# The second layer's experts with weights in 8 KB runs, gate and up on the two halves of the array, and the features stored in that order

## The chip, the cores and the metric

The kernel runs on one core of one Trainium2 chip. The metric is the device time of one launch in microseconds (us), as the median of the runs shown. All data is fp32 in DRAM; products run on TensorE (PE), elementwise work on VectorE (DVE), ScalarE (ACT) and GpSimd (POOL), and loads are issued from SyncE's queue (SP).

## What is computed

A backbone of two layers: each mixes tokens by four kinds of attention and then passes them through a hierarchical mixture of 16 gated experts, of which every token uses two. The second layer handles 256 latent tokens. What matters here is its mixture:

```python
eid = grp[:, None] * EXPERTS_PER_GROUP + top_i          # two experts of a token
gate = jnp.einsum('nke,nk->ne', one_hot(eid, N_EXPERTS), w_top)
y = jnp.zeros(hf.shape)                                 # hf: (256, 1024), normed, scaled and shifted
for e in range(N_EXPERTS):                              # 16
    a = silu(hf @ w_gate[e]) * (hf @ w_up[e])           # w_gate, w_up: (1024, 512)
    y = y + gate[:, e:e + 1] * (a @ w_down[e])          # w_down: (512, 1024)
```

The weights of one layer's experts are 16 x 3 x 2 MB, and each is read once.

## The kernel before, in words

`moe(l, ...)` holds the mixture of a layer; the second layer takes the path `half`. Its weights are read as 96 tiles of 1 MB into a ring of 15 places (`RING[1]`), in the order of the list `todo` (L1145 to L1149): gate in two tiles (the first and the second 512 of its 1024 rows), up in two, then down of the expert before in two. `load_expert` (L1120) issues each as one DMA on SP: row 128k + p of the tile goes to partition p as its k-th piece, so that a partition takes runs of 2 KB (a row of gate or up) or 4 KB (a row of down). A DMA is issued once its place in the ring is free.

The tokens, normed but not yet scaled and shifted, are kept as two float32r parts `xhat` (L1224 on ACT, L1225 and L1226 on POOL). `half_experts` (L1475) works on them. `tables` (L1491), for four experts at a time, gathers the tokens of each expert by products with one-hot rows (L1505), applies scale and shift feature by feature (`modulate`, L264 and L266, with `mod2`), and leaves `X`, feature-major, with room for 64 tokens an expert; L1511 makes the tokens' weights and L1519 the transposed one-hot rows.

`expert` (L1539) is a generator with these steps, all of PE's work in fp32:

- gate and up (L1547): per 128 features, X's 64 tokens are the stationary operand and weights the moving one; columns 0 to 255 go to the lower half of the array, columns 256 to 511 to the upper half, so that a product is 64 x 256, 32 of them an expert;
- SiLU on ACT (L1551) and the product with up on DVE (L1552), 128 x 256 each;
- two transposes of 128 x 128 (L1556) and a copy on ACT (L1558);
- down (L1564): 8 products of 64 x 512, again with halves of the columns on halves of the array; then weighting on DVE (L1567) and a split in two float32r parts (L1569 on ACT, L1570 on DVE);
- the combining products (L1576), 8 of 128 x 512, which add the expert's rows to the tokens' sums in PSUM.

The loop at L1592 interleaves experts: gate of e, combine of e-2, up of e, down of e-1, transposes of e. Then a scheduler with its own estimate of durations orders the instructions of each engine; the order on PE, fixed at build time, is thus neither the loop's nor the programmer's. After the last expert a norm follows and the output is stored (L1697 to L1711).

In the trace a fp32 product of PE is recorded as two MATMUL instructions, so that "x16" in a row of the trace is 8 products of the program.

## Time and profile before

| | us |
|---|---|
| runs shown | 1304.49, 1299.95, 1298.3 (median 1299.95) |
| profiled execution, span from first to last instruction | 1302.6 |
| second layer's experts, first table product to the last combining product | 1043.3 to 1289.8 |
| PE busy | 1146.7 (88%) |
| DVE busy | 793.7 (61%) |
| ACT busy | 559.1 (43%) |
| POOL busy | 254.3 (20%) |

The page gives the profiled execution's span and no separate device time for it; the span lies between the three runs, 2.65 us above their median. The profile is read here mostly by its timeline: start of a merged run of like instructions, its length, engine, line, operation, tiles, shape and count. A run's length contains the draining of its last product, so that the time a run takes up on PE is read from its start to the next run's start.

### The profile page before, as it was taken

What the parts mean: (1) busy time and instruction counts of PE and PEld (TensorE: products, weight loads), DVE (VectorE), ACT (ScalarE), POOL (GpSimd) and SP (SyncE); (2) the same over time, 40 slices, a digit from 0 to 9 for tenths busy, and PEclk for the clock granted to TensorE, in tenths of its full rate; (3) what the DMA queues carried; (4) which work ended last, traced back from release to release, by engine and by line L of the source; (5) the groups of instructions that cost most, each with busy time, mean ns of one, the idle gap of its engine ahead of it and who ended that gap; (6) DMA issues with size and microseconds to landing.
All of it is one profiled execution on the core that took longest, in us unless ns stands there. A gap on an engine that the chain in (4) does not pass through costs nothing. (4 is left out here: it accounts for less than half of the span.)

```text
span 1302.6 us, 16444 instructions
## 1 busy us (share of the span) xinstructions
PE 1146.7 (88%) x5920; PEld 770.1 (59%) x5920; DVE 793.7 (61%) x1676; ACT 559.1 (43%) x951; POOL 254.3 (20%) x235
## 2 busy tenths in 40 slices
PE   5999999899945999989999978998989589999995
PEld 2777644367833777767777647654457455455552
DVE  4377156674797899979888688735874711211113
ACT  2332155664325677767677444415553311111110
POOL 0022011222132344435352205120001200000000
PEclk9999969989967899999999979997979789999998
DMA  9933546701567899999998453542723979999993
GB/s 351 311 106 83 188 171 236 241 12 34 202 226 250 284 328 346 336 330 352 307 319 276 175 176 119 153 162 106 259 84 101 329 244 395 393 394 394 394 394 138
DMA packets 151770, 315.77 MB, mean 242 GB/s; under 512 B 21295, under 2 KB 36405, under 8 KB 146560
## 3 DMA queue, kind: packets, MB, share of 16 engines
q1 hardware_dynamic: 146868, 305.96, 66.9%
q0 software_dynamic: 4560, 8.57, 1.8%
q8 instruction: 49, 0.80, 0.3%
q14 instruction: 41, 0.34, 0.1%
q10 hardware_dynamic: 252, 0.09, 0.0%
HBM read 307.28 MB, written 15.27 MB: 248 GB/s over the span
## 5 line engine op out<-in xcount | busy, mean ns | idle before, releaser
L1360 DVE TENSOR_TENSOR hl<-rb,hl 128x1024 fp32r<-128x1024 f32 x127 | 189.7, 1520 | 30.6 <-ACT hl L1358 30.3
L1358 ACT ACTIVATE hl<-rb 128x1024 fp32r<-128x1024 f32 x152 | 158.0, 1058 | 69.8 <-PE mm L1370 63.3
L1370 PE MATMUL mm<-hl,t 128*128 128x512 f32 x256 | 106.0, 414 | 3.2 <-DVE hl L1360 3.2
L1371 PE MATMUL mm<-hl,t 128*128 128x512 f32 x256 | 102.9, 402 | 4.5 <-DVE t L1389 4.3
L1369 PE MATMUL mm<-hl,t 128*128 128x512 f32 x256 | 103.0, 407 | 1.1 <-ACT t L1388 1.1
L1547 PE MATMUL mm<-rb,xt 128*64 128x256 f32 x816 | 101.0, 383 | 0.0
L563 PE MATMUL mm<-s,hh 128*128 128x512 f32 x216 | 88.1, 412 | 0.0
L565 PE MATMUL mm<-s,hh 128*128 128x512 f32 x216 | 87.9, 410 | 0.0
L564 PE MATMUL mm<-s,hh 128*128 128x512 f32 x216 | 87.0, 403 | 0.0
L1547 PEld LDWEIGHTS mm<-rb,xt 128*64 128x64 f32 x816 | 58.1, 137 | 35.3 <-issue 8.8
L1360 POOL TENSOR_TENSOR hl<-rb,hl 128x1024 fp32r<-128x1024 f32 x25 | 70.1, 2815 | 24.2 <-ACT hl L1358 23.5
L824 ACT ACTIVATE e<-mm,nmx 128x512 f32<-128x512 f32 (+1 forms) x96 | 58.4, 616 | 29.3 <-DVE nmx L819 16.3
L819 DVE TENSOR_REDUCE nmx<-mm 128x1 f32<-128x512 f32 (+1 forms) x80 | 52.7, 684 | 11.1 <-PE mm L813 10.3
L1371 PEld LDWEIGHTS mm<-hl,t 128*128 128x128 f32 x256 | 49.7, 194 | 16.2 <-DVE t L1389 6.7
L1370 PEld LDWEIGHTS mm<-hl,t 128*128 128x128 f32 x256 | 49.7, 194 | 14.7 <-DVE hl L1360 5.2
L1552 DVE TENSOR_TENSOR ta<-ta,mm 128x256 f32<-128x256 f32 x16 | 6.7, 421 | 84.4 <-ACT ta L1551 84.4
L1369 PEld LDWEIGHTS mm<-hl,t 128*128 128x128 f32 x256 | 49.7, 194 | 12.1 <-ACT t L1388 2.0
L1369 PE MATMUL mm<-hl,at 128*128 128x512 f32 x128 | 53.0, 414 | 3.7 <-ACT at L1408 3.7
L1371 PE MATMUL mm<-hl,at 128*128 128x512 f32 x128 | 50.2, 411 | 6.0 <-DVE at L1409 5.7
L833 POOL TENSOR_SCALAR e<-e,rc 128x256 f32<-128x256 f32 x32 | 30.0, 950 | 128.7 <-DVE rc L831 98.5
L1370 PE MATMUL mm<-hl,at 128*128 128x512 f32 x128 | 52.9, 413 | 1.5 <-DVE hl L1360 1.2
L424 ACT ACTIVATE s<-ra 128x1024 fp32r<-128x1024 f32 x30 | 31.3, 1059 | 51.4 <-PE mm L565 25.5
(494 smaller groups left out, 2437.4 us busy)
## 6 DMA issues: line engine op xcount, KB each, us to landing
rb<-in_moe_w_up_dram SPq DMA_DIRECT2D x52, 1024.0 KB
rb<-in_moe_w_down_dram SPq DMA_DIRECT2D x50, 1024.0 KB
rb<-in_moe_w_gate_dram SPq DMA_DIRECT2D x49, 1024.0 KB
ra<-in_w_ada_dram SPq DMA_DIRECT2D x40, 1024.0 KB
ra<-in_moe_w_gate_dram SPq DMA_DIRECT2D x14, 1024.0 KB
ra<-in_w_in_dram SPq DMA_DIRECT2D x24, 512.0 KB
ra<-in_moe_w_down_dram SPq DMA_DIRECT2D x11, 1024.0 KB
ra<-in_moe_w_up_dram SPq DMA_DIRECT2D x9, 1024.0 KB
```

The costliest lines, as they stand in the source:

```text
L424: S.activation(hi, w, AF.Copy)
L563: T.matmul(ps, a, hi[:, k2], start=k == 0, stop=False)
L564: T.matmul(ps, a, lo[:, k2], start=False, stop=False)
L565: T.matmul(ps, b, hi[:, k2], start=False, stop=k == KD - 1)
L819: V.tensor_reduce(nmx[:, :nb], ps, axis=AX, op=ALU.max, negate=True)
L824: S.activation(e[:, b], ps[:, b], AF.Exp, bias=nmx[:, b:b + 1], accum_out=sm[:, b:b + 1])
L1358: S.activation(hi, w[k2], AF.Copy)
L1360: eng.tensor_tensor(lo, w[k2], hi.bitcast(F32), op=ALU.subtract)
L1369: T.matmul(ps[:C], ah, hs[:, k2], start=first and k2 == 0, stop=False)
L1370: T.matmul(ps[:C], ah, ls[:, k2], start=False, stop=False)
L1371: T.matmul(ps[:C], al, hs[:, k2], start=False, stop=last and k2 == 1)
L1547: T.matmul(ps[64 * t:64 * t + 64, j], X[:, k, gi], wt, start=k == 0, stop=k == KD - 1)
```

## The change

The tile of gate or up now puts rows 4p to 4p+3 of its 512 into partition p, one run of 8 KB; down puts rows 2p and 2p+1 of its 256 there, also 8 KB. The contraction index of a product is thereby another set of features, so the features of `xhat` are stored in that order (ACT and POOL write or read with a step of 128 elements), scale and shift get a third copy `mod2[:, 2]` in that order (a 4 x 512 load and four small transposes, once), and the activations' columns are taken with a step of 2 in the transposes. Gate now works on the lower half of the array and up on the upper half, both over all 512 columns: 16 products of 64 x 512 an expert instead of 32 of 64 x 256, and the load order is gate, up, gate, up. SiLU and the product with up are 64 x 512 instead of 128 x 256; four transposes of 64 x 128 take the place of two of 128 x 128. Cut to its core (comments and the path for overfull experts, which does not run, left out):

```diff
-        V.tensor_copy(mod2, ps[:, 0:32].rearrange("p (s r) -> p s r", s=2))
+        V.tensor_copy(mod2[:, 0:2], ps[:, 0:32].rearrange("p (s r) -> p s r", s=2))
         V.tensor_copy(lnb, ps[:, 32:40])
+        if not full:
+            r4 = P3("r4", [4, 512])
+            SY.dma_start(r4, modD[l][0:1, 1024:3072].rearrange("s (r p) -> (s r) p", p=512))
+            ps = tr([128, 4, 4])
+            for j in range(4):
+                T.transpose(ps[:, j], r4[:, j::4], ident[0:4, 0:4])
+            V.tensor_copy(mod2[:, 2].rearrange("p (r j) -> p j r", j=4), ps)
...
-            src = src.rearrange("(k p) n -> p k n", p=128)
+            src = src.rearrange("(p k) n -> p k n" if half else "(k p) n -> p k n", p=128)
...
-            for n, d in (("gate", 0), ("up", 0), ("down", 1)) if half else (("up", 1), ("gate", 0), ("down", 1)):
+            if half:
+                todo += [(e, f"moe_w_{n}", i) for i in range(2) for n in ("gate", "up") if e < E]
+                todo += [(e - 1, "moe_w_down", i) for i in range(2) if e > 0]
+                continue
+            for n, d in (("up", 1), ("gate", 0), ("down", 1)):
...
-                    S.activation(xhat[0][:, ch], x, AF.Identity, scale=rstd2[:, c:c + 1], bias=nb[:, c:c + 1])
+                    hi, lo = (t[:, ch].rearrange("p (h j q) -> p h q j", h=2, j=4) for t in xhat)
+                    xv, xhv = (t.rearrange("p (h q j) -> p h q j", h=2, j=4) for t in (x, xh))
+                    S.activation(hi, xv, AF.Identity, scale=rstd2[:, c:c + 1], bias=nb[:, c:c + 1])
                     G.tensor_scalar(xh, x, rstd2[:, c:c + 1], nb[:, c:c + 1], op0=ALU.mult, op1=ALU.add)
-                    G.tensor_tensor(xhat[1][:, ch], xh, xhat[0][:, ch].bitcast(F32), op=ALU.subtract)
+                    G.tensor_tensor(lo, xhv, hi.bitcast(F32), op=ALU.subtract)
...
-                ps = mm([128, 2, 256])
-                for j, n in enumerate(("moe_w_gate", "moe_w_up")):
-                    for kh in range(2):
-                        for kt, wt in enumerate(pieces(e, n, kh)):
-                            k, t = 4 * kh + kt // 2, kt % 2
-                            T.matmul(ps[64 * t:64 * t + 64, j], X[:, k, gi], wt, start=k == 0, stop=k == KD - 1)
-                    if j == 0:
+                ps = mm([128, 512])
+                for kh in range(2):
+                    both = [pieces(e, f"moe_w_{n}", kh) for n in ("gate", "up")]
+                    for k in range(4 * kh, 4 * kh + 4):
+                        for t in range(2):
+                            T.matmul(ps[64 * t:64 * t + 64], X[:, k, gi], next(both[t]),
+                                     start=k == 0, stop=k == KD - 1)
+                    if kh == 0:
                         yield
-                a = PX("ta", [128, 256], bufs=2)
-                S.activation(a, ps[:, 0], AF.Silu)
-                V.tensor_tensor(a, a, ps[:, 1], op=ALU.mult)
+                a = PX("ta", [64, 512], bufs=2)
+                S.activation(a, ps[0:64], AF.Silu)
+                V.tensor_tensor(a, a, ps[64:128], op=ALU.mult)
                 yield
-                pt = tr([128, 2, 128])
-                for k in range(2):
-                    T.transpose(pt[:, k], a[:, 128 * k:128 * k + 128], ident)
-                aT = PX("at", [128, 2, 128], bufs=2)
+                pt = tr([128, 4, 64])
+                for k in range(4):
+                    T.transpose(pt[:, k], a[:, 256 * (k // 2) + k % 2:256 * (k // 2) + 256:2], ident[0:64, 0:64])
+                aT = PX("at", [128, 4, 64], bufs=2)
```

The scheduler also orders PE's instructions anew. The first place is PE in the last four experts, where one expert follows another with nothing else between. In the rows `mm` is the sum of gate and up, `mx` that of down; `rb`, `ra` and `x` are weight tiles; `y` and `ohT` belong to the combining products and `tr<-cst,ta` are the transposes; "x8" is a count of products. Before, around the gate and up products of expert 13 (`mm_10826`), from the last combining product of expert 12 on:

```order
L1576 MATMUL mm_9255<-y_10818,ohT_10195 128x512
L1547 MATMUL mm_10826<-rb_2498_10651,xt_10525 64x256 x8
L1547 MATMUL mm_10826<-rb_2499_10657,xt_10525 64x256 x8
L1547 MATMUL mm_10826<-ra_10675,xt_10525 64x256 x8
L1564 MATMUL mx_10878<-ra_10685,at_10824 64x512 x4
L1556 MATMUL tr_10895<-cst,ta_10875 128x128 x2
L1564 MATMUL mx_10878<-rb_2508_10703,at_10824 64x512 x4
L1547 MATMUL mm_10900<-rb_2509_10713,xt_10525 64x256 x8
L1576 MATMUL mm_9252<-y_10891,ohT_10581 128x512
```

With the change, from the transposes of expert 12 into the products of expert 13 (`mm_10606`):

```order
L1572 MATMUL tr_10599<-cst,ta_10577 128x64 x4
L1580 MATMUL mx_10580<-x_2480_10441,at_10542 64x512 x4
L1562 MATMUL mm_10606<-rb_2481_10444,xt_10347 64x512
L1591 MATMUL mm_9260<-y_10595,ohT_10073 128x512
...
L1562 MATMUL mm_10606<-rb_2484_10457,xt_10347 64x512
L1562 MATMUL mm_10606<-rb_2481_10444,xt_10347 64x512
L1562 MATMUL mm_10606<-rb_2484_10457,xt_10347 64x512
```

Before, eight products of an expert (four on each half of the array) stand between the down products of the expert before it and that expert's eight combining products, and 24 stand behind these. Now one product (gate's first, on the lower half) stands ahead and 15 stand behind, which begin with one on the upper half (`rb_2481` holds gate, `rb_2484` up).

The second place is PE while the tables of the last four experts are made (`tr<-oh,xhat`). Before:

```order
L1505 MATMUL tr_10537<-oh_10516,xhat_7864 128x256
L1547 MATMUL mm_10598<-x_2444_10347,xt_10139 64x256 x8
L1547 MATMUL mm_10598<-rb_2451_10365,xt_10139 64x256 x7
L1505 MATMUL tr_10526<-oh_10516,xhat_7863 128x256
L1505 MATMUL tr_10526<-oh_10516,xhat_7864 128x256
```

With the change:

```order
L1519 MATMUL tr_10359<-oh_10338,xhat_7863 128x256
L1519 MATMUL tr_10359<-oh_10338,xhat_7864 128x256
L1562 MATMUL mm_10420<-x_2430_10195,xt_10017 64x512
L1519 MATMUL tr_10348<-oh_10338,xhat_7863 128x256
L1519 MATMUL tr_10348<-oh_10338,xhat_7864 128x256
```

A run of 15 products between table products has become a run of one. Over all 16 experts the runs of gate and up products, taken between products of other lines, number 50 with 512 products before, 16 of them of an odd count, and 46 with 256 products now, 32 of them of an odd count. Down has 24 runs before and 26 now, two of an odd count in each. Changes of kind on PE, with down and gate or up in a row counted as one kind, number 126 before and 119 now.

## Rows read from the trace of the kernel before

**Rows 1.** Page, part 1: busy time, share of the span and instructions of each engine.

```profile
PE 1146.7 (88%) x5920; PEld 770.1 (59%) x5920; DVE 793.7 (61%) x1676; ACT 559.1 (43%) x951; POOL 254.3 (20%) x235
```

**Rows 2.** Stretches: us; busy of PE, PEld, DVE, ACT, POOL; PE clock; DMA share; GB/s.

```profile
1010.00:1020.00 10.00, 5.74 (x28) 4.69 (x27) 7.98 (x20) 3.68 (x6) 0.00 (x0) 0.86 1.04 386
1090.00:1270.00 180.00, 177.03 (x1261) 97.06 (x1260) 32.59 (x68) 26.90 (x60) 0.00 (x0) 1.00 1.04 394
1270.00:1275.00 5.00, 4.88 (x42) 2.90 (x42) 0.69 (x1) 0.18 (x1) 0.00 (x0) 1.00 1.03 411
1275.00:1280.00 5.00, 5.00 (x36) 2.23 (x34) 0.42 (x1) 0.77 (x2) 0.00 (x0) 1.00 0.67 270
```

**Rows 3.** Who PE waited for, 1046 to 1290 us: us in total, times, longest.

```profile
PE tr L1556 <- DVE ta L1552: 4.0, 3, 1.9
PE mm L1576 <- ACT y L1569: 1.6, 1, 1.6
```

**Rows 4.** Timeline of PE in expert 12: start, us, line, tiles, shapes, count.

```profile
1231.25 1.90 PE L1547 MATMUL mm<-rb,xt 128*64 128x256 f32 x16
1233.08 1.38 PE L1576 MATMUL mm<-y,ohT 64*128 64x512 f32 x8
1234.39 5.40 PE L1547 MATMUL mm<-rb,xt 128*64 128x256 f32 x48
1239.62 1.89 PE L1564 MATMUL mx<-rb,at 128*64 128x512 f32 x8
1241.44 0.44 PE L1556 MATMUL tr<-cst,ta 128*128 128x128 f32 x2
1241.80 1.94 PE L1564 MATMUL mx<-x,at 128*64 128x512 f32 x8
1243.57 1.90 PE L1547 MATMUL mm<-rb,xt 128*64 128x256 f32 x16
```

**Rows 5.** Timeline of PE, one product alone between two runs of combining products.

```profile
1081.51 0.65 PE L1547 MATMUL mm<-rb,xt 128*64 128x256 f32 x2
1082.08 0.73 PE L1576 MATMUL mm<-y,ohT 64*128 64x512 f32 x4
```

**Rows 6.** Timeline of PE, products with one column and their 128-column loads.

```profile
1102.24 1.95 PE L1511 MATMUL tr<-rt,oh 128*128 128x1 f32 x16
1104.05 0.42 PE L1519 MATMUL tr<-cst,oh 128*128 128x128 f32 x2
```

**Rows 7.** Timeline of PE, the last down and combining products.

```profile
1281.87 1.94 PE L1564 MATMUL mx<-ra,at 128*64 128x512 f32 x8 [0.90 <-issue]
1284.87 1.94 PE L1564 MATMUL mx<-ra,at 128*64 128x512 f32 x8
1288.38 1.46 PE L1576 MATMUL mm<-y,ohT 64*128 64x512 f32 x8 [1.58 <-ACT y L1569]
```

**Rows 8.** Timeline of DVE and ACT, what the last combining products need.

```profile
1286.86 0.75 DVE L1567 SCALAR_TENSOR_TENSOR oh<-mx,tw,junk 128x512 f32<-128x512 f32 x1 [3.63 <-PE mx L1564]
1287.70 0.63 ACT L1569 ACTIVATE y<-oh 128x512 fp32r<-128x512 f32 x1 [5.20 <-DVE oh L1567]
1288.36 0.69 DVE L1570 TENSOR_TENSOR y<-oh,y 128x512 fp32r<-128x512 f32 x1 [0.76 <-ACT y L1569]
```

**Rows 9.** Timeline of ACT and DVE, 128x256 in the experts, 64x512 in attention.

```profile
1064.69 0.38 ACT L1551 ACTIVATE ta<-mm 128x256 f32<-128x256 f32 x1
1065.10 0.42 DVE L1552 TENSOR_TENSOR ta<-ta,mm 128x256 f32<-128x256 f32 x1 [8.47 <-ACT ta L1551]
945.74 0.59 ACT L800 ACTIVATE st<-tr 64x512 fp32r<-64x512 f32 x1
947.34 0.68 DVE L802 TENSOR_TENSOR st<-tr,st 64x512 fp32r<-64x512 f32 x1
```

**Rows 10.** Timeline of POOL and DVE ahead of the routing.

```profile
1029.35 4.64 POOL L1226 TENSOR_TENSOR xhat<-r,xhat 128x1024 fp32r<-128x1024 f32 x2
1029.66 4.35 DVE L1260 TENSOR_TENSOR rt<-lgt,rt 128x32 f32<-128x32 f32 x2
```

More of the change, by code (lines that the diff above doesn't have):

```diff
@@ L1506, in tables @@
                                          start=ch + j == 0, stop=ch + j == nch)
-                        modulate(X[:, k], ps[:, k2], mod2, 0, k)
+                        modulate(X[:, k], ps[:, k2], mod2, 2, k)
                 ps = tr([128, 512])
@@ L1527, in pieces @@
                     wt = weights(e, n, i)
-                for k in range(2 if down else 4):
-                    r = 256 * i + 128 * k if down else 512 * i + 128 * k
-                    for t in range(2):
+                R = 256 if down else 512
+                for k in range(R // 128):
+                    for t in range(2 if down else 1):
                         if isinstance(e, int):
-                            yield wt[k][:, 0, 512 * t:512 * t + 512] if down else wt[k // 2][:, k % 2, 256 * t:256 * t + 256]
+                            yield wt[k][:, 0, 512 * t:512 * t + 512] if down else wt[k // 2][:, k % 2]
                             continue
-                        m = 512 if down else 256
-                        w = PX("hl", [128, 512])[:, :m]
-                        SY.dma_start(w, I[n][l, ds(e, 1)].rearrange("a k n -> (a k) n")[r:r + 128, m * t:m * t + m])
+                        w = PX("ta", [128, 512], bufs=2)
+                        src = I[n][l, ds(e, 1)].rearrange("a k n -> (a k) n")[R * i:R * i + R, 512 * t:512 * t + 512]
+                        SY.dma_start(w, src.rearrange("(p k) n -> p k n", p=128)[:, k])
                         yield w
@@ L1563, in expert @@
                         k, t = kt // 2, kt % 2
-                        T.matmul(ps[64 * t:64 * t + 64], aT[:, k, 64 * i:64 * i + 64], wt,
-                                 start=i + k == 0, stop=i + k == 2)
+                        T.matmul(ps[64 * t:64 * t + 64], aT[:, 2 * i + k], wt, start=i + k == 0, stop=i + k == 2)
                 y = PX("oh", [128, 512])
@@ L1727, in kern @@
     for l in range(L):
-        mod2 = cp.tile([128, 2, 16], F32, name=f"mod2{l}")
+        mod2 = cp.tile([128, 2 + l, 16], F32, name=f"mod2{l}")
         later = vectors((0, 1), (0, 2), (1, 0)) if l == 0 else vectors((1, 1), (1, 2))
```

## The prediction

> **What bounds the kernel now.** I read the busy shares first, then the stretch of the second layer's experts: its DMA rate, who PE waits for, and PE's timeline there.
>
> By busy time PE leads with 1146.7 us of 1302.6 [rows 1], but that is a mean over stages. In the 180 us from 1090 to 1270 two things are full at once: PE is busy for 177.03 us and the DMA engines show a share of 1.04 at 394 GB/s [rows 2]. Which of the two sets the end decides everything here, since the change is made to the transfers and to PE's products alike. Two readings say PE.
>
> First, PE never waits for a weight: the two large entries of its waits between 1046 and 1290 us are 4.0 us for the transposes' input from DVE and 1.6 us for the last combining products' input from ACT [rows 3]; no entry names a DMA. Second, the weights land early. The transfers end within the stretch 1275 to 1280, at a share of 0.67, so near 1278.4 [rows 2]; the last 1 MB of them are the norm's two rows, 2.6 us at 411 GB/s, so that the last weight lands near 1275.8. PE starts on it at 1284.87 [rows 7], 9 us later. Expert 12's first gate tile has 25 tiles behind it, 2.66 us each at 394 GB/s, and so lands near 1209; PE takes it at 1231.25 [rows 4], 22 us later. PE uses a tile every 12.34 / 6 = 2.06 us there (expert 12's gate starts at 1231.25, expert 13's at 1243.57) and the transfers bring one every 2.66 us: the ring was full before PE began, PE eats the lead up, and 9 us of it are left at the end. The transfers run all the time and are still not what PE waits for.
>
> **What PE's time is made of.** From expert 12 [rows 4]: 8 gate products, 4 on each half of the array, take 1.83 us from their start to the next run; 24 take 5.23 us. So a pair (one product on each half, at the same time) takes (5.23 - 1.83) / 8 = 0.425 us, and a change of kind 1.83 - 4 x 0.425 = 0.13 us. Four down products of 512 columns take 1.82 and 1.77 us, two pairs: 0.85 us a pair with the change taken off. Twice the columns, twice the time: nothing is left that fewer, wider products could save but the changes of kind.
>
> **The change, part by part**, against the profiled span of 1302.6 us; a difference found there is then put on the median of the runs, 1299.95.
>
> *Gate and up, sixteen wide products.* In pairs they would take 8 x 0.85 = 6.8 us an expert, the same as 16 x 0.425 before. But a product that stands alone between other kinds takes as long as a pair: one of 256 columns between two runs of combining products took 0.57 us [rows 5], which is 0.425 + 0.13, its partner half idle. The new order has many such runs: a run of n products takes (n + 1) / 2 pairs, rounded down, and over the 16 experts that makes 144 pairs of 0.85, 122.4 us, where there were 264 of 0.425, 112.2 us. Both counts are sums over the runs of the two orders (46 and 50 runs). **+10.2 us.** In the steady pattern it is easily seen: 1 + 15 products take 1 + 8 pairs, not 8. Down keeps 65 pairs. Changes of kind fall from 126 to 119: **-0.9 us.** Where a lone product follows or precedes down on the other half, it may overlap; two or three places, **-0.5 us.**
>
> *Transposes.* Four instead of two an expert, each with 128 stationary columns and 64 moving ones instead of 128. Sixteen one-column products, each with a 128-column load, take 1.81 us [rows 6], 0.113 us each, so the load sets their time. The two old transposes take 0.36 us with a change of kind [rows 4], 0.115 each. If the load sets it, 32 more cost 32 x 0.11 = 3.5 us; if the moving columns set it, four short ones cost what two long ones did, 0. I take **+3.5 us**, since the load's row is the nearest, and keep 0 as the other end. The stationary operand has 64 partitions instead of 128, and no row here shows what that does to a load; the Trainium skill (TensorE: Matmul & The Clock Gate, section on LDWEIGHTS) says that a load goes by its columns and not by its partitions. By that rule, at 128 / 1.2 = 107 ns, the term would be 3.4 us (an estimate).
>
> *Combining products behind a short cover.* They need the down sum weighted on DVE and rounded on ACT: at the end of the kernel 3.51 us pass from the start of the last four down products (1284.87) to the combining products (1288.38), 0.75 on DVE and 0.63 on ACT among them [rows 7, 8]. In expert 12 the four down products (1.77) and eight gate products (1.83) lie between, 3.60 us, and cover it. Now it is 1.77 and one lone product, 0.85 + 0.13: 2.75 us, 0.76 short. The second four need the other part, which DVE ends at 1289.05, 4.2 us after that start, and lose another 0.1 or so; some of that is lost before too. I count 0.7 us at the six places where the new order has down, one gate product, combining products: **+4.2 us.** Everything behind waits too, as PE takes its instructions in order: 15 products whose data is there.
>
> *SiLU and the product with up.* 0.38 and 0.42 us become, by the rows of the same shape in attention, 0.59 and 0.68 [rows 9]; with the gaps the chain is some 1.4 us. The new order puts four down products (1.77 us) ahead of nearly every expert's transposes, which hides it. Before, three transposes stood bare and cost 4.0 us [rows 3]; now I find only the first expert's, which is behind a table load on ACT, at 1.8: **-2.2 us.** If that cover were gone, it would be 1.4 us at each place.
>
> *Ahead of the experts.* The 4 x 512 load joins SP's queue behind two small ones, and the loads behind it go some 0.4 us later, long before their use; four small transposes and a copy, once: **+0.5 us.** ACT's and POOL's work on `xhat` now steps by 128 elements. POOL's subtraction, 2 x 2.3 us, counts: DVE's 128x32 products stood for 4.35 us and ended with it, and the routing behind them is the way to the first expert [rows 10]. No row shows such a step; the ends are 0 (same time) and double (+4.7). I take **0**, as every element is still one read and one write, and keep 4.7 for the range.
>
> *The transfers.* Runs of 8 KB may well go faster: 2 KB runs alone went at 386 GB/s (1010 to 1020), 4 KB runs alone at 411 (1270 to 1275) [rows 2]. That lengthens a lead that nobody waits for. Gate and up tiles alternate; the first ten are there before PE starts. Cost and gain 0; the cover is the 9 us of lead, and PE gets later, not earlier.
>
> Sum: 10.2 - 0.9 - 0.5 + 3.5 + 4.2 - 2.2 + 0.5 = **+14.8 us**, 1317.4 for the profiled span and **1314.7** on the median.
>
> **The rivals.**
>
> *The transfers were the bound after all (faster).* For it: a share of 1.04 for 180 us. The saturated stretch is some 203 us (1075 to 1278). At 411 GB/s it shrinks by 203 x (1 - 394/411) = 8.4 us; drawn on by the line through 2 and 4 KB (84.9 and 159.5 ns a run and engine of 16, so 10.3 ns a run besides its bytes, 308.7 ns for 8 KB, 425 GB/s) by 14.8. That gives 1285 to 1291.5. It decides only if a tile lands after PE wants it, that is if PE were more than 9 us faster; rows 3 and 7 speak against it. The Trainium skill (Perfetto Trace Analysis, section DMA Optimizations) calls larger runs, 2 KB to 4 or 8 KB, the primary step where a DMA-bound kernel shows high utilization. The trace agrees on the rate, 386 against 411, but not that the kernel is DMA-bound.
>
> *The lone products cost little (no change).* If the array's idle half took up the next kind's products, the 10.2 us would go, with transposes at the moving columns' price (0): -0.9 - 0.5 + 4.2 - 2.2 + 0.5 leaves +1.1, 1301; with 3.5 for the transposes 1304.5. Against it stands the one lone product of rows 5, and the 0.13 us at each change of kind.
>
> *POOL's stepped subtraction doubles (slower still).* 1314.7 + 4.7 = 1319.4; it decides from any lengthening on, as DVE waits to its end.
>
> *The change doesn't do what it says:* the runs are 8 KB by the shape of the DMAs (128 x 2048), so only the rate is open, which is the first rival.
>
> **How the numbers follow.** The forecast, 1314.7, has 0.65; its own terms reach from 1309 (transposes at 0, the wait behind down at half) to 1318. POOL's rival has 0.13, the lone products for nothing 0.14, the transfers 0.08. A measurement here can tell about 0.5%, 6.5 us, from no change: slower is above 1306.5, so 0.65 + 0.13 = 0.78; same is the second rival, 0.14; faster 0.08. The range takes in the forecast, POOL's rival with the spread of the runs on top (1322) and the second rival's upper half (1303).
>
> **What would show it.** Right: between 1090 and 1290 PE as busy as before but with an expert every 14 us or so at the end (12.34 + 0.85 + 0.22 + 0.7) instead of 12.34; DMA share under 1 there, the ring being full; in the steady pattern a lone gate product with 0.98 us to the combining products or a wait for ACT there; 0.58 us for four transposes. Wrong: waits of PE for a weight tile; combining products that start while the lone product still runs; an expert in 12.5 us or less.

## The result, and the profile after

1313.48 us, the median of seven runs, against 1300.25, the median of seven runs of the kernel before beside them: a ratio of 1.011, 95% interval 1.007 to 1.014. The forecast was 1314.7. One of the seven runs, at 1659 us with a mean granted clock of 0.64, was a slow one; it counts in the median (1312.74 without it) and not in the ratio. The profiled execution has a span of 1319.3 us where that of before had 1302.6.

Page of the changed kernel, part 1 (busy time, share, instructions), beside [rows 1]:

```profile
PE 1160.8 (88%) x5444; PEld 741.5 (56%) x5444; DVE 799.8 (61%) x1677; ACT 564.0 (43%) x951; POOL 255.9 (19%) x235
```

PE has 476 recorded MATMUL instructions fewer (a fp32 product is two of them) and is busy 14.1 us longer. The same stretches as in [rows 2], same columns:

```profile
1010.00:1020.00 10.00, 6.05 (x26) 4.51 (x25) 5.01 (x9) 2.21 (x3) 0.00 (x0) 1.00 1.01 421
1090.00:1270.00 180.00, 175.10 (x827) 70.39 (x826) 34.37 (x65) 27.32 (x57) 0.00 (x0) 1.00 0.97 390
1270.00:1275.00 5.00, 4.53 (x24) 1.73 (x26) 0.69 (x1) 0.42 (x1) 0.00 (x0) 1.00 1.00 418
1275.00:1280.00 5.00, 5.00 (x25) 1.64 (x22) 0.39 (x1) 0.59 (x1) 0.00 (x0) 1.00 0.69 279
1280.00:1285.00 5.00, 4.28 (x18) 1.58 (x18) 1.34 (x3) 1.01 (x2) 0.00 (x0) 1.00 0.00 0
```

The transfers did get faster, 421 GB/s for 386 where they run alone, and it bought nothing: over the 180 us they move 390 GB/s, at a share that fell from 1.04 to 0.97, since they wait longer for places in the ring: from 1040 to 1290 SP's queue stood 133.1 us until gate and up products gave one free, 89.6 us before. They end at the same time as before, near 1278, while PE starts on the last weight at 1301.31 (timeline of PE, its last two rows of this stage):

```profile
1301.31 1.94 PE L1580 MATMUL mx<-ra,at 128*64 128x512 f32 x8
1304.82 1.46 PE L1591 MATMUL mm<-y,ohT 64*128 64x512 f32 x8 [1.57 <-ACT y L1584]
```

The lead of 9 us [rows 7] has become some 25. Who PE waited for, 1040 to 1310 us (us in total, times, longest), beside [rows 3]:

```profile
PE mm L1591 <- ACT y L1584: 5.9, 7, 1.6
...
PE tr L1519 <- DVE oh L1511: 4.0, 2, 3.2
PE tr L1533 <- ACT ohT L1534: 1.0, 1, 1.0
```

No transfer is in the list. The combining products waited once before and wait seven times now; the transposes of the activations no longer wait for DVE. PE's steady pattern at the end, beside [rows 4]:

```profile
1243.37 6.65 PE L1562 MATMUL mm<-rb,xt 128*64 128x512 f32 x29
...
1252.10 0.69 PE L1572 MATMUL tr<-cst,ta 64*128 64x64 f32 x4
1252.72 1.94 PE L1580 MATMUL mx<-x,at 128*64 128x512 f32 x8
1254.48 1.02 PE L1562 MATMUL mm<-rb,xt 128*64 128x512 f32 x2
1256.23 1.46 PE L1591 MATMUL mm<-y,ohT 64*128 64x512 f32 x8 [0.72 <-ACT y L1584]
1257.62 3.65 PE L1562 MATMUL mm<-rb,xt 128*64 128x512 f32 x16
```

An expert takes 14.25 us (1243.37 to 1257.62) instead of 12.32. The last three rows show why: one gate product stands alone at 1254.48 (the row counts two records for it) and holds PE for 1.03 us, a pair and a change of kind; then PE waits 0.72 us for the part that ACT rounds. Ahead of the experts, ACT, POOL and DVE in one stretch:

```profile
1030.27 4.22 ACT L1238 ACTIVATE xhat<-x,nb,rs_yc 128x1024 fp32r<-128x1024 f32 x2 [1.91 <-DVE nb L1224]
1032.78 5.69 POOL L1240 TENSOR_TENSOR xhat<-r,xhat 128x1024 fp32r<-128x1024 f32 x2
1033.09 5.39 DVE L1274 TENSOR_TENSOR rt<-lgt,rt 128x32 f32<-128x32 f32 x2
1043.20 1.66 DVE L1511 TENSOR_SCALAR oh<-cst,rt 128x128 fp32r<-128x128 f32 x8 [1.05 <-PEq L1630]
```

The stepped rows cost POOL 1.05 us and DVE, which stands until POOL ends, 1.04 [rows 10]; ACT takes 4.22 us where it took 2.37. The last line is the first thing behind the jump over the loop for overfull experts; in the kernel before, the same wait is 3 us longer:

```profile
1041.67 1.66 DVE L1497 TENSOR_SCALAR oh<-cst,rt 128x128 fp32r<-128x128 f32 x8 [3.99 <-PEq L1615]
```

**Where the 16.7 us between the two spans lie.** The experts' stage, first table product to the end of the last combining products, went from 246.6 to 261.5: +14.9. From the router's last products (start 1023.48 and 1026.95) to the first table it went from 19.80 to 17.86: +1.0 for the stepped rows, -2.9 at the jump. 3.5 us had come up before the router already, in code that differs by one small load, four small transposes and the transfers of the first weights. The last part of the kernel is as long as it was (12.8 and 13.0 us). The part ahead of the router scatters: in the fourteen traces of this study, one of each kernel, the router's last products start between 1011.8 and 1031.0 us. Hence the experiments are compared by the length of the experts' stage and by the time from one expert to the next first, and by the median of the runs second.

### The profile page after: what moved, and what is told of

It is laid out like the page before. It is cut to its first block, busy times and chain, and to the rows that moved or that the text cites. A ratio compares the mean times of both kernels' runs of the same rounds, so it can differ in the third digit from the quotient of the medians.

```text
span 1319.3 us, 15512 instructions
## 1 busy us (share of the span) xinstructions
PE 1160.8 (88%) x5444; PEld 741.5 (56%) x5444; DVE 799.8 (61%) x1677; ACT 564.0 (43%) x951; POOL 255.9 (19%) x235
## 5 line engine op out<-in xcount | busy, mean ns | idle before, releaser
L1562 PE MATMUL mm<-rb,xt 128*64 128x512 f32 x408 | 117.4, 601 | 0.0
L1568 DVE TENSOR_TENSOR ta<-ta,mm 64x512 f32<-64x512 f32 x16 | 11.0, 690 | 97.0 <-ACT ta L1567 97.0
L1562 PEld LDWEIGHTS mm<-rb,xt 128*64 128x64 f32 x408 | 32.9, 137 | 55.2 <-issue 54.2
L819 DVE TENSOR_REDUCE nmx<-mm 128x1 f32<-128x512 f32 (+1 forms) x80 | 52.7, 683 | 11.3 <-PE mm L813 10.5
L1374 DVE TENSOR_TENSOR hl<-ra,hl 128x1024 fp32r<-128x1024 f32 x33 | 46.6, 1437 | 11.9 <-ACT hl L1372 10.5
```

Of the source, the lines that this page charges most:

```text
L819: V.tensor_reduce(nmx[:, :nb], ps, axis=AX, op=ALU.max, negate=True)
L1374: eng.tensor_tensor(lo, w[k2], hi.bitcast(F32), op=ALU.subtract)
L1562: T.matmul(ps[64 * t:64 * t + 64], X[:, k, gi], next(both[t]), start=k == 0, stop=k == KD - 1)
```

## The experiments

**pairs_kept, one_alone, two_together: PE's order.** The steps of the experts are put into a fixed order for PE; only the place of the combining products differs between the three. (The lines taken out and the last three put in are left out; the comments are added here.)

```diff
+            with in_order(mybir.EngineType.PE):
+                tabs, runs = [group(0)], []
+                for e in range(E):
+                    runs.append(expert(tabs[e // 4], e % 4, e, e == E - 1))
+                    next(runs[e])                      # 8 products (one_alone: 1, two_together: 2)
+                    if e == 1:
+                        next(runs[0])                  # transposes of the first expert
+                    if e > 1:
+                        next(runs[e - 2], None)        # combining products
+                    next(runs[e])                      # the rest of 16, SiLU
+                    if e % 4 == 2 and e + 2 < E:
+                        tabs.append(group(e + 2))      # next four experts' tables
+                    if e > 0:
+                        next(runs[e - 1])              # down
+                        next(runs[e])                  # transposes
```

> The changed kernel, with only the order of PE's instructions in the second layer's experts written down: 8 gate and up products, the eight combining products of the expert two before, the other 8 products, (every fourth expert the next tables,) eight down products, four transposes. No run of products is odd and eight products (3.5 us) stand between an expert's down products and its combining products. Theory (PE is the bound, and the change's cost sits in lone products, in combining products behind too short a cover and in changes of kind): against the kernel before 128 pairs of 0.853 us for 264 of 0.4265 is -3.4, one down pair less -0.85, 81 runs of a kind for 138 at 0.13 us -7.4, 32 more transposes +3.4, waits of 5.6 us down to about 2 is -3.6, and +1.5 for what lies ahead of the experts: about 1290 us, and an expert every 12.5 us in the steady pattern instead of 14.25. Rival one (the 512-column products on the two halves, or the stepped writes of the features, cost the time by themselves): still 1308 to 1314, an expert every 14 us. Rival two (the transfers are the bound): 1300 or more whatever PE's order, with waits of PE for weight tiles.

> As pairs_kept, but the combining products come after the first of the sixteen gate and up products, so that 15 times one product stands alone and 15 follow in a row. Theory (a lone product takes a whole pair's time): 15 more pairs of 0.853 us than pairs_kept, +12.8 us, and +1 to +3 of waits for the combining products' input, since transposes (0.56) and one product (0.98) instead of eight products (3.5) now lie behind the down products: 1303 to 1306 us, an expert every 13.3 to 13.5 us. Rival (the idle half is taken up by the combining products, a lone product costs only its own 0.43): +0 to +3 against pairs_kept, 1290 to 1293.

> As one_alone, but the combining products come after the first two products. The cover behind the down products is as long as with one (a lone product is supposed to take as long as a pair), so only the oddness of the runs differs. Theory: 128 pairs as in pairs_kept, so 12.8 us less than one_alone, and +1 to +3 of waits against pairs_kept: 1291 to 1293 us, an expert every 12.5 to 12.7 us. Rival (lone products cost little): the same time as one_alone. If the wait for the combining products were the larger part of the change's cost, both would be slower than pairs_kept by the same amount.

| | us, median | ratio to before | stage | an expert |
|---|---|---|---|---|
| before (stage and expert from the trace above) | 1301.34 | 1 | 246.6 | 12.32 |
| change (ratio to the runs of before beside it) | 1313.48 | 1.011 (1.007 to 1.014) | 261.5 | 14.25 |
| pairs_kept | 1314.08 | 1.009 (1.006 to 1.012) | 256.6 | 12.35 |
| two_together | 1316.70 | 1.014 (1.009 to 1.019) | 264.8 | 12.89 |
| one_alone | 1329.66 | 1.020 (1.014 to 1.025) | 275.8 | 13.75 |

PE in one_alone, where one product stands ahead of the combining products:

```profile
1255.02 1.07 PE L1562 MATMUL mm<-rb,xt 128*64 128x512 f32 x2
...
1256.81 0.96 PE L1591 MATMUL mm<-y,ohT 64*128 64x512 f32 x6 [0.23 <-DVE y L1585]
1257.70 6.65 PE L1562 MATMUL mm<-rb,xt 128*64 128x512 f32 x29
...
1268.15 0.69 PE L1572 MATMUL tr<-cst,ta 64*128 64x64 f32 x4
```

and in two_together, where two do:

```profile
1235.27 1.08 PE L1562 MATMUL mm<-rb,xt 128*64 128x512 f32 x4
1236.33 0.50 PE L1591 MATMUL mm<-y,ohT 64*128 64x512 f32 x2
1237.06 0.96 PE L1591 MATMUL mm<-y,ohT 64*128 64x512 f32 x6 [0.23 <-DVE y L1585]
1237.94 6.23 PE L1562 MATMUL mm<-rb,xt 128*64 128x512 f32 x28
...
1247.54 0.69 PE L1572 MATMUL tr<-cst,ta 64*128 64x64 f32 x4
```

One product holds PE for 1.07 us and two for 1.08, the wait behind is the same 0.23, and the odd run behind it needs a pair more: 13.75 - 12.89 = 0.86 us an expert, one pair of 0.85. That a lone product costs a whole pair is shown. So is the short cover: two_together and pairs_kept have the same pairs, and 12.89 - 12.35 = 0.54 us an expert is what the combining products lose when two products instead of eight lie behind the transposes. In pairs_kept the eight combining products take 1.13 us to the next run's start,

```profile
1252.07 1.20 PE L1591 MATMUL mm<-y,ohT 64*128 64x512 f32 x8
1253.20 3.65 PE L1562 MATMUL mm<-rb,xt 128*64 128x512 f32 x16
```

in two_together 1.61 (1236.33 to 1237.94): the wait of 0.23 breaks them after two, and 0.25 more goes with the break.

The totals missed their expectations all the same, all three by some 24 us: pairs_kept was to take 1290. Its steady part is as fast as that of the kernel before, and its tables eat the gain. PE at the second of the four tables:

```profile
1099.02 1.21 PE L1519 MATMUL tr<-oh,xhat 128*128 128x256 f32 x8 [0.66 <-ACT xt L264]
...
1103.34 1.84 PE L1525 MATMUL tr<-rt,oh 128*128 128x1 f32 x16
1105.04 1.90 PE L1533 MATMUL tr<-cst,oh 128*128 128x128 f32 x8
1106.87 3.42 PE L1580 MATMUL mx<-rb,at 128*64 128x512 f32 x8
1110.12 1.88 PE L1580 MATMUL mx<-x,at 128*64 128x512 f32 x8
```

Made in one block, the tables' products wait 16 times 0.66 us for ACT to read the tile that they write the other half of (10.5 us in all), and the first four down products behind them take 3.25 us where the next four take 1.82: the granted clock was 0.66 from 1105 to 1110, part of the time at its lower level of 1.2 GHz, after those waits, the one-column products and the transposes in a row. From the first table (1048.8) to 1065 it was 0.50 throughout. The scheduler's order had put other products between, and had lone ones for it.

**products_only: the change without its transfers.**

```diff
-            src = src.rearrange("(p k) n -> p k n" if half else "(k p) n -> p k n", p=128)
+            src = src.rearrange("(k p) n -> p k n", p=128)
...
-                    T.transpose(pt[:, k], a[:, 256 * (k // 2) + k % 2:256 * (k // 2) + 256:2], ident[0:64, 0:64])
+                    T.transpose(pt[:, k], a[:, 128 * k:128 * k + 128], ident[0:64, 0:64])
```

The stepped rows, the third slice of shift and scale and the loop for overfull experts follow suit.

> The change without its transfers: weights with their rows 128 apart (runs of 2 and 4 KB) as before, the features in their own order (no stepped writes, no third slice of the shift and scale), but gate and up on the two halves, 16 products of 512 columns, and four transposes of 64 rows as in the change. PE's order is as in the change up to small pieces: 145 pairs instead of 144, 130 runs of a kind instead of 133. Theory (PE): as slow as the change, less the 1.5 to 2 us of the stepped writes, 1308 to 1314 us. Rival (the transfers, the features' order or the stepped writes are what made the change slower): back to 1298 to 1302.

1306.39 us (10 runs), ratio 1.006 (1.003 to 1.009), between the two expectations. The stage says which holds: 259.7 us, 1.8 less than the change, 13.1 more than before. In the profiled execution the part up to the router was 12 us shorter than the change's, by the scatter named above. The 1.8 us are not what I had named, the stepped rows, which lie ahead of the stage; four transposes take 0.39 us here instead of 0.62. That led to unstep, below.

**packed: tables in pieces.** pairs_kept, with the tables' steps between the products, and the two reads of a table's PSUM tile after both of its halves (the core of it):

```diff
                             T.matmul(ps[:, k2], xhat[j][:, ch, 128 * k:128 * k + 128], oh[:, ch, :, 0:C],
                                      start=ch + j == 0, stop=ch + j == nch)
-                        modulate(X[:, k], ps[:, k2], mod2, 2, k)
+                    for k2 in range(2):
+                        modulate(X[:, 2 * kp + k2], ps[:, k2], mod2, 2, 2 * kp + k2)
+                    yield
```

> The changed kernel with PE's order in the experts written down as in pairs_kept, and two things more: the tables of the next four experts are made in pieces of 8 or 16 products between runs of 4 or 8 gate and up products (pairs_kept made them in one block of 56, which in its trace waited 16 times 0.66 us for ACT and was followed by products at half the granted clock), and ACT and DVE read the two halves of a table's PSUM tile after both are there. Transfers, features and products are those of the change. Theory (the change's cost is PE's order: lone products, short covers, and in pairs_kept the bare tables): first table to last combining products 236 to 242 us, against 246.6 in the kernel before, 261.5 in the change and 256.6 in pairs_kept; 1288 to 1296 us in all, an expert every 12.35 us. Rival (wide products on the two halves, or what comes with them, cost by themselves): a stage of 250 or more, 1303 or more.

1287.75 us (6 runs), ratio 0.988 (0.983 to 0.993); stage 235.2 us, an expert every 12.35. That is the theory's outcome, a shade better than its 236 to 242 and 1288 to 1296: the change's transfers, features and wide products, and 26 us less in the stage by PE's order and the later reads of the tables' tiles. Which of these two is worth how much was not tried. The wide products are not dear in themselves.

**before_packed, loads_packed: the products of before in that order**, without and with the change's transfers. In loads_packed the features stand in their own order and the tables read every fourth:

```diff
-                                T.matmul(ps[:, k2], xhat[j][:, ch, 128 * k:128 * k + 128], oh[:, ch, :, 0:C],
+                                T.matmul(ps[:, k2], xhat[j][:, ch, 512 * (k // 4) + k % 4:512 * (k // 4) + 512:4], oh[:, ch, :, 0:C],
```

> The kernel before (products of 256 columns, 2 and 4 KB runs, two transposes) with the same written order as packed. Theory (PE is the bound, 9 us ahead of the last weight): the order takes some 12 us out of PE's 246.6 us, more than the lead of 9 us, so that PE now waits for weight tiles at the end: 1290 to 1293 us, with waits for a DMA in the list of PE's waits. If the transfers were no bound even then: 1287 to 1289 us without such waits. Rival (the order of before cost nothing): 1298 to 1302.

> The products of the kernel before (256 columns, two transposes an expert) in the written order of packed, with the change's transfers in 8 KB runs; the features stand in their own order in their rows, and the tables' products read every fourth of them, so that ACT and POOL write no stepped rows. Theory: PE's time as in before_packed (some 234 us a stage), and no wait for a weight, since 8 KB runs at 420 GB/s end some 13 us before the 394 GB/s of before: 1284 to 1288 us, 3 to 6 less than before_packed; that difference is what the transfers are worth once PE no longer hides them. Rival (longer runs are worth nothing here): the same as before_packed. If products with every fourth feature as the stationary operand took longer, it would show as more than 1.2 us for eight of the tables' products.

before_packed: 1290.42 us (8 runs), ratio 0.991 (0.988 to 0.995), stage 236.9. Its waits, 1020 us to the end, now name transfers:

```profile
PE mx L1575 <- DMA rb<-in_moe_w_down_dram: 1.8, 3, 0.7
PE mm L1558 <- DMA rb<-in_moe_w_gate_dram: 1.3, 2, 0.7
...
PE mm L1558 <- DMA rb<-in_moe_w_up_dram: 0.4, 1, 0.4
```

The last experts take 12.97 and 16.04 us instead of 12.13. So the lead of 9 us was read rightly: take some 12 us from PE's work, and the weights are late.

loads_packed missed its 1284 to 1288: 1301.52 us (12 runs), ratio 1.000 (0.996 to 1.003). An expert takes 12.20 us and no transfer is waited for, but the stage takes 247.4. Its table products, by line and form (busy, mean ns), and sixteen of them up to the next run:

```profile
L1520 PE MATMUL tr<-oh,xhat 128*128 128x256 f32 x121 | 30.4, 407 | 0.0
1043.86 4.01 PE L1520 MATMUL tr<-oh,xhat 128*128 128x256 f32 x16
1047.80 1.96 PE L1572 MATMUL mm<-rb,xt 128*64 128x256 f32 x16
```

and those of packed:

```profile
L1522 PE MATMUL tr<-oh,xhat 128*128 128x256 f32 x122 | 17.6, 298 | 0.0
1129.91 2.15 PE L1522 MATMUL tr<-oh,xhat 128*128 128x256 f32 x16
1132.00 1.94 PE L1573 MATMUL mm<-rb,xt 128*64 128x512 f32 x8
```

These products are of float32r and have one record each. Sixteen take 3.94 us instead of 2.09 from start to next start: a stationary operand that is read with a step of four elements costs 0.12 us more a product, some 15 us for 128. The stepped rows of `xhat`, 1 us once, are what the change pays to be spared that. The Trainium skill (SBUF — State Buffer, section Door 1: The DMA port swizzle) has lines of 16 bytes, and a price for each read that crosses to a new one; four float32 fill one, and the trace agrees that such a step has a price. The same passage has four float32 as how far a step is free, and there the trace differs.

**loads_only: the change's transfers with the products of before**, order left to the scheduler (the products as in before, `pt[:, k]` from `a[:, k::2]`).

> The change's transfers (8 KB runs), its stored order of the features (stepped writes of ACT and POOL, third slice of shift and scale), but products as before: 256 columns, gate first, then up, two transposes; PE's order is left to the scheduler and is as before up to small pieces (264 pairs, 140 runs of a kind for 138). Theory (PE is the bound): as before, plus 1 us for the stepped writes: 1299 to 1304 us, though the weights land 13 us earlier. Rival one (the transfers are the bound): 1285 to 1292. Rival two (the transfers or the features' order made the change slower): 1308 or more.

1306.96 us (12 runs), ratio 1.005 (1.002 to 1.008); stage 248.7, an expert every 12.38. No gain, though the transfers end near 1273 us instead of 1278, as PE's bound has it; but the time lies between the expected 1299 to 1304 and the second rival's 1308. Of the profiled execution's 3.7 us over that of before (spans 1306.3 and 1302.6) 2.1 lie in the stage and 1.4 between the router and the first table, 1.0 of it by the stepped rows and 0.5 at the jump described below. The two stepped transposes (0.43 us instead of 0.37) are 16 x 0.06 = 1.0 of the 2.1. So 2 us of the second rival are shown, by the steps; the medians lie 7.3 us apart, and the rest is not shown.

**unstep, packed_unstep: the transposes' step.** DVE writes the product with up in the order of the weights' rows:

```diff
-                V.tensor_tensor(a, a, ps[64:128], op=ALU.mult)
+                b = PX("ta", [64, 512], bufs=2)
+                u, v = (t.rearrange("p (i q k) -> p i k q", i=2, k=2) for t in (a, ps[64:128]))
+                V.tensor_tensor(b.rearrange("p (i k q) -> p i k q", i=2, k=2), u, v, op=ALU.mult)
+                a = b
...
-                    T.transpose(pt[:, k], a[:, 256 * (k // 2) + k % 2:256 * (k // 2) + 256:2], ident[0:64, 0:64])
+                    T.transpose(pt[:, k], a[:, 128 * k:128 * k + 128], ident[0:64, 0:64])
```

> The change with nothing but the transposes' step taken away, as in packed_unstep; PE's order is the scheduler's again and moves a little (145 pairs for 144, 129 runs of a kind for 133). Theory: 0.39 instead of 0.62 us for four transposes, -3.7 us for sixteen experts, about the same lone products and short covers: 1307 to 1312 us. Rival: 0.62 us still, 1312 to 1315.

> As packed, but DVE writes the product with up already in the order of the weights' rows, so that the four transposes read 128 neighbouring elements as their stationary operand instead of every second one. In the traces so far four transposes take 0.62 us to the next product's start with the step (the change) and 0.39 without (products_only), and two of 128 rows 0.37 without and 0.43 with it (before, loads_only). Theory (it is the step of the stationary operand that makes the transposes dear, not that there are four): 0.39 us for four, an expert every 12.12 us, 16 x 0.23 = 3.7 us less than packed: a stage of about 232 us and 1283 to 1286 us. Rival (four loads cost their time however they are stored, as the prediction had it): 0.58 to 0.62 us for four, 12.35 an expert and the time of packed.

PE in packed_unstep:

```profile
1220.22 0.46 PE L1586 MATMUL tr<-cst,ta 64*128 64x64 f32 x4
1220.61 3.65 PE L1573 MATMUL mm<-rb,xt 128*64 128x512 f32 x16
...
1232.35 0.46 PE L1586 MATMUL tr<-cst,ta 64*128 64x64 f32 x4
```

0.39 us for four transposes, 12.12 an expert, stage 231.7 (packed: 235.2), all as expected. DVE's 64x512 product takes 0.69 us with the step in its output as without. The weight loads of the transposes (`PEld`), without the step, with it (packed), and in the kernel before (loads, busy, mean ns):

```profile
L1586 PEld LDWEIGHTS tr<-cst,ta 64*128 64x128 f32 x64 | 5.1, 137 | 13.0 <-issue 13.0
L1583 PEld LDWEIGHTS tr<-cst,ta 64*128 64x128 f32 x64 | 8.8, 208 | 13.0 <-issue 13.0
L1556 PEld LDWEIGHTS tr<-cst,ta 128*128 128x128 f32 x32 | 3.3, 140 | 13.0 <-DVE ta L1552 8.2 <-issue 4.4 <-ACT y L1569 0.4
```

A load with 64 partitions takes as long as one with 128; the step is what lengthens it.

The total is 1278.78 us (6 runs), ratio 0.987 (0.981 to 0.992), the lowest of the study. It is below the expected 1283 to 1286, and not all of the 20 us to the kernel before are shown to be the order's and the step's: the stage is 14.9 us shorter, and in the profiled execution another 8.3 lie ahead of the router, where all kernels scatter. In unstep an expert takes 14.02 us instead of 14.25, as the theory has it; the total, 1318.86 (4 runs, 1306.3 to 1325.2), ratio 1.011 (1.005 to 1.018), is above the expected 1307 to 1312 and says nothing of the step, since the scheduler put the one-column products and transposes of one table in a row (stage 265.0, the granted clock at 0.83 from 1100 to 1120).

**products_packed: what 8 KB runs are worth in the end.** packed with the changes of products_only.

> As packed, but with the weights' rows 128 apart (2 and 4 KB runs) and the features in their own order, as in the kernel before: PE has the work of packed_unstep, the transfers are those of the kernel before. Theory: the transfers at 394 GB/s are now the bound at the end: PE waits for weight tiles from about the twelfth expert on, as in before_packed, 1288 to 1292 us, 4 to 7 more than packed_unstep, and that is what 8 KB runs are worth in this kernel. Rival (the transfers are worth nothing even now): the time of packed_unstep or, for the rows that needn't be stored in steps, 1 us less, 1282 to 1285.

1283.75 us (6 runs), ratio 0.989 (0.985 to 0.993), below the expected 1288 to 1292 and within the rival's 1282 to 1285; but the rival wanted packed_unstep's time, and the distance to it came out as the theory has it: stage 236.6 (before_packed: 236.9) against 231.7, medians 5.0 apart. PE's work is the same, 12.12 us an expert, and in the list of its waits stands

```profile
PE mm L1562 <- DMA rb<-in_moe_w_up_dram: 3.1, 2, 1.6
```

The stretch 1100 to 1240 in products_packed:

```profile
1100.00:1240.00 140.00, 138.41 (x716) 56.13 (x713) 29.30 (x56) 23.43 (x46) 0.00 (x0) 1.00 1.04 394
```

and in packed_unstep:

```profile
1100.00:1240.00 140.00, 140.00 (x722) 56.15 (x720) 29.32 (x56) 23.55 (x46) 0.00 (x0) 0.99 1.01 420
```

The 8 KB runs are worth 4.9 us of the stage, from the moment on that PE is fast enough to want them.

**before_short_loop: the jump.**

```diff
-                            T.matmul(ps[64 * t:64 * t + 64, j], X[:, k, gi], wt, start=k == 0, stop=k == KD - 1)
+                            if isinstance(e, int) or k in (0, 1, 6, 7):
+                                T.matmul(ps[64 * t:64 * t + 64, j], X[:, k, gi], wt, start=k == 0, stop=k == KD - 1)
```

> The kernel before, with half of the gate and up products left out of the loop for experts with more than 64 tokens, which is jumped over with these inputs (its result would be wrong for other ones): 16 instead of 32 products of PE in the loop's code, as many as in the change. It asks where 3 us went that nobody had asked for: in the kernels with 256-column products DVE stands for 3.99 us at the jump, with 512-column ones for 1.05. Theory (the length of PE's code that is jumped over sets it): about 1.05 us here, and the first table 3 us earlier than in the kernel before. Rival (it is something else that the wide products bring): 3.99 still.

DVE behind the jump:

```profile
1038.02 1.66 DVE L1497 TENSOR_SCALAR oh<-cst,rt 128x128 fp32r<-128x128 f32 x8 [0.98 <-PEq L1616]
```

0.98 us instead of 3.99, the stage as before (246.7). In the fourteen traces the wait is 3.99 to 4.46 us in the four kernels with 32 products in that loop and 0.98 to 1.05 in the ten with 16. Code that never runs had cost 3 us by its length. One run, 1300.81 us, can't show 3 us in the total.

## Why the prediction was right

The time (1314.7 against 1313.5) and its mechanism hold: PE bounds the stage, PE's order makes the wide products dear, and the transfers' gain has no taker. That the time is so near is in part luck: the stage was forecast at +14.3 and came to +14.9, while ahead of it +0.5 became -1.9; the 13.0 of the two together is what the medians show (1313.48 - 1300.25 = 13.2). The expert's 12.34 us in the working is 12.32 by its own two starts, which changes nothing. By its own terms:

- *Lone products and odd runs, +10.2.* Right. one_alone against two_together gives 0.86 us for a product without a partner, 0.85 in the working; 144 pairs, where the old 264 of half the width come to 132, is 12 of them.
- *Combining products behind a short cover, +4.2.* Right: six waits of 0.72 us, 5.9 less the last one's 1.6 that was there before [rows 3], is 4.3.
- *SiLU and transposes' waits, -2.2.* The 4.0 us of waiting for DVE's product went altogether; 1.0 for the transposed one-hot rows, just ahead of the first expert's transposes, came: -3.0.
- *Transposes, +3.5.* Right in size (16 x (0.62 - 0.36) = 4.2) by luck, and wrong in its reason. I had put the price on the number of loads, with the moving columns (0) as the other end. products_only and packed_unstep show 0.39 us for four loads that lie together: the end of 0 was the truth for the count, and the 0.23 an expert comes from the step of two that the 8 KB rows of down bring with them. The diff showed the step, and I gave it no row. The row that I took [rows 6], sixteen records with one moving column, is eight products with two loads each; its 0.113 us a load was not the price here. Without the step four loads lie within 5.1 / 16 = 0.32 us, four transposes with 64 moving columns take (0.39 - 0.13) / 4 = 0.065 us each, and the two old ones with 128 took 0.115. That fits the moving columns; the partitions are halved too, and no run parts the two. The Trainium skill's rule (TensorE: Matmul & The Clock Gate, section on LDWEIGHTS), by columns and not by partitions, gives four loads 4 x 107 ns (an estimate). The trace agrees that the partitions make no difference (137 and 140 ns), and not that the loads add up. The Trainium skill (SBUF — State Buffer, section Door 1: The DMA port swizzle) has two hits in a line of 16 bytes as enough for full speed, which a step of two float32 gives; 208 against 137 ns a load and 0.62 against 0.39 us differ from that too.
- *Ahead of the experts, +0.5, and POOL's step at 0.* Mis-sized: POOL +1.05, by which DVE and the routing are later, +1.0 in all. That is between the ends of 0 and 4.7; the rival that doubled it is refuted. ACT's stepped write, not counted at all, took 4.22 us for 2.37 and stayed beside the path.
- *What was not in the sum:* -2.9 us at the jump, which before_short_loop puts on the length of the loop's code.
- *Changes of kind, -0.9, and the overlap, -0.5,* were not measured apart. With them the stage's terms come to 10.2 + 4.3 - 3.0 + 4.2 - 0.9 - 0.5 = 14.3 of the 14.9 us; 0.6 stays open. PE's waits for the tables' inputs grew by about as much: 0.9 us for one-hot rows (the second of the two times above) where it was 0.4, and 0.7 for ACT's features where it was 0.4.
- *The rivals.* The transfers as the bound: refuted by loads_only, where the 8 KB runs alone bring no gain, and settled by products_packed, where they do once PE has been made some 15 us faster. The forecast of 425 GB/s by the line through 2 and 4 KB came near: 418 to 421. Lone products for little: refuted by one_alone. Of the signs named ahead, the expert every 14 us, the share under 1 and the wait for ACT behind the lone product came; the four transposes took 0.62 us for 0.58, by the step. None of the signs of being wrong came.

The order forced in pairs_kept shows where such reasoning goes wrong: I priced the runs and forgot that tables in one block wait for their readers, and that the clock fell behind them. The expectation missed by 24 us; packed, with the tables in pieces and their reads later, came out at 1288.

## What to carry to other kernels

Where an array is split into halves, count the odd runs in the order that is really issued: a product without a partner cost a pair here, and it was the order's choice of where to cut, not the width of the products, that decided (stage 261.5 us for the change, 235.2 for packed). A faster transfer shows only after the engine that hides it has been sped up, so change the two in that order, and read the lead (when the last weight lands, when it is first used) before either. When a layout is changed for the transfers' sake, follow the step it leaves in every operand to the end, and let an engine off the path take it: as PE's stationary operand it cost 15 us in loads_packed and 3.5 in packed, in DVE's output nothing that shows.

## What was not expected of the hardware

- A stationary operand with a step: four float32, 0.12 us more for each of the 128-column loads of the tables (3.94 us for sixteen instead of 2.09); two float32, 0.62 us instead of 0.39 for four transposes, 0.43 instead of 0.37 for two of 128 rows. The same step written by DVE left its product at 0.69 us (packed_unstep).
- Rows written with a step of 128 elements: ACT 2.21 us a 128x1024 instead of 1.23, POOL 2.87 instead of 2.32, half of [rows 10].
- Jumping over a loop: DVE stood 3.99 to 4.46 us for PE's sequencer with 32 products in its code for PE, 0.98 to 1.05 with 16. The Trainium skill (Runtime: NRT & Kernel Launch, section Instruction fetch mechanics) has a taken branch beyond what is already fetched wait for the fetch; that shortening the code alone took 3 us of the wait away agrees; where the limit lies was not tried.
